# ConvFFN of a two-layer trunk: TensorE in source order, weight sums behind the previous pair, the first block's down products one pair later

## The chip, the cores and the metric

The kernel runs on one core of a Trainium2 chip. The metric is the device time of one execution in microseconds (us). A core has engines that each work through their own queue of instructions in order: TensorE (PE, with its weight loads as PEld), VectorE (DVE), ScalarE (ACT), GpSimd (POOL) and SyncE (SP). They meet at semaphores. PSUM, into which TensorE writes, has eight banks here, each a tile of 128 x 512 float32.

## The reference

The input is x of shape (1, 512, 1024), in float32. Two layers follow each other. Each is a token mixer and a feed-forward network (FFN); the change touches the FFN, which both layers have.

```python
for i in range(DEPTH):                       # DEPTH = 2
    h = rmsnorm(x, norm_mix_g[i])
    x = x + (gla_mixer(h, ...) if i % 2 == 0 else short_conv_mixer(h, ...))
    h = rmsnorm(x, norm_ffn_g[i])
    x = x + conv_ffn(h, ffn_w_up[i], ffn_conv_w[i], ffn_w_down[i])
return rmsnorm(x, final_norm_g)

def conv_ffn(h, w_up, conv_w, w_down):       # w_up 1024 x 5632, w_down 2816 x 1024
    up = causal_dwconv(h @ w_up, conv_w)     # three taps over the positions
    a, u = up[..., :D_FF], up[..., D_FF:]
    return (jax.nn.silu(a) * u) @ w_down
```

## The kernel before

**Tiling.** Channels lie on the 128 partitions and the 512 positions in the free dimension. The hidden layer of the FFN has 22 tiles j of 128 channels, each with a part a (`i = 0`) and a part u (`i = 1`). A product of float32 matrices is made of three matmuls on split operands: the high part (`h`) times the high part, high times low (`l`) and low times high. So each product of 128 x 128 weights comes as three matmuls.

**Weights.** Each weight tile is loaded raw by SP (L124, tile `wr`, a ring of 6 buffers), then split into `wh` and `wl` (mostly rings of 4). `halve` (L129) makes `wh` by a cast on ScalarE. It makes `wl` either by a subtraction on VectorE (L135) or, for units marked `added`, by a negated copy on ScalarE (L132) and an accumulating DMA that GpSimd issues (L133). `take` hands out one unit, and each call also starts the split of the unit three places further on. A raw buffer can be loaded again only when the split of what it held is done, and the loads wait in SP's queue in their order.

**Pairs.** Tiles j from 4 on are made in pairs of weight tiles (parts a and u of one j) by seven half-width products in place of eight. `seven_first` (step `s1`, 48 matmuls of 256 columns, PSUM tiles `updc` and `upab`) takes two units, `seven_last` (step `s2`, 36 matmuls) takes two more. The four units are sums and differences of the raw weights, made on VectorE in `forms`: `s` (L144) and L146 for the first unit, L150 and L151 for the later ones. In `seven_first` VectorE makes `e` (L671), the difference of two of the products. Behind `seven_last` VectorE and ScalarE make the two up tiles, the norm's factor (L696), the convolution (`conv3`, L365 to L367), the gate (L701, L702) and the split result `g<j>`.

**Plain tiles.** Tiles 0 to 3 are plain products of 24 matmuls of 512 columns (`up` both parts, `ua` part a, `ub` part u). Part u of tile 3 (`ub 3`) comes in the middle of pair 6.

**Down products.** The 22 tiles are cut into four blocks (0 to 5, 6 to 10, 11 to 15, 16 to 21). A step `dn b m` multiplies block b's tiles `g` by the weights of output tile m (18 matmuls of 512 columns for six tiles, 15 for five) and adds the result to `x[m]` (L715). The eight steps of a block are put between the pairs of the block behind it, by `ff_steps`. `dn 0 0` is called the first down group below. It is the first user of `g3`, the gate of tile 3.

**What sets the order.** The source says in which order the work is written down. Within that, the framework's scheduler decides each engine's order by its own idea of when operands are ready, so an instruction that stands later in the source can come earlier in a queue. `tc.issue_after(ins)` puts the instructions of a block behind `ins` on its engine; `tc.manual_schedule(engines=...)` keeps the source's order on the engines that it names.

The functions that the diff touches:

Of the kernel before, what the change touches and what calls it, by code (L numbers as in the profile page):

```python
# [18 lines left out]
KD = D // P  # L19
# [10 lines left out]
HALVED = 4  # L30
# [5 lines left out]
def trunk_kernel(ctx, tc, xT, w_qk, w_v, w_g, w_up_gate, b_gate, w_go, w_sc, w_so, w_up, w_dn,  # L36
                 smalls, ff_cw, out):
    nc = tc.nc
    V, S, G, PE = nc.vector, nc.scalar, nc.gpsimd, nc.tensor
# [9 lines left out]
    def ps(name):  # L49
        return psp.tile([P, T], F32, tag="ps", name=name)  # L50

    def wk(name, shape=(P, T), dt=F32, bufs=2, tag=None, pool=work):
        return pool.tile(list(shape), dt, tag=tag or name, name=name, bufs=bufs)
# [5 lines left out]
    def bt(tag, name, shape=(P, T), dt=F32):  # L59
        return big.tile(list(shape), dt, tag=tag, name=name)  # L60
# [20 lines left out]
    class Weights:  # L81
# [3 lines left out]
        def __init__(self):  # L85
            self.units, self.srcs, self.need, self.last = [], [], [], []
            self.raw, self.split, self.hold = {}, {}, {}
            self.paired, self.added = set(), set()

            self.anchors = ()  # L90
            self.nl = self.ns = self.ng = 0

        def add(self, src, added=False):
# [43 lines left out]
        def forms(self, n, q, h, l):  # L137


            ra, rb = self.raw[n], self.raw[n + 1]  # L140
            lo, hi = slice(0, T), slice(T, 2 * T)
            if q == 0:
                s3 = bt(f"b13{'hl'[n % 4 // 2]}", f"s{n}")
                V.tensor_add(s3, ra[:, lo], rb[:, lo])  # L144
                self.halve(h[:, lo], l[:, lo], s3)
                V.tensor_add(rb[:, lo], rb[:, lo], rb[:, hi])  # L146
                self.halve(h[:, hi], l[:, hi], rb[:, lo])
            elif q == 1:
                self.halve(h, l, ra)
                V.tensor_add(ra[:, lo], ra[:, lo], rb[:, lo])  # L150
                V.tensor_add(ra[:, hi], ra[:, hi], ra[:, lo])  # L151
            elif q == 2:
                self.halve(h, l, rb[:, hi])
            else:
                self.halve(h, l, ra)
# [38 lines left out]
        def take(self):  # L194

            for _ in range(2):
                if self.nl < len(self.srcs) and (self.nl < 6 or self.last[self.nl - 6] < self.ns):
                    self.load()
                    if self.nl not in self.paired:
                        break  # L200
            self.part()
            self.ng += 1
            return self.split.pop(self.ng - 1)

    W = Weights()
# [7 lines left out]
    def ff_steps():  # L213
        steps = [("up", 0), ("up", 1), ("ua", 2), ("s1", 4), ("ub", 2), ("s2", 4), ("s1", 5), ("ua", 3), ("s2", 5)]

        middle = [("ub", 3)]
        for b in range(1, len(BLOCKS)):
            j0, j1 = BLOCKS[b]
            dn = [("dn", b - 1, m) for m in range(KD)]
            for j in range(j0, j1):  # L220
                steps += [("s1", j), middle.pop() if j == j0 else dn.pop(0), ("s2", j)]
                if j1 - j < len(dn) or j == j0 and b > 1:
                    steps.append(dn.pop(0))
            middle = dn
        return steps + middle + [("dn", len(BLOCKS) - 1, m) for m in range(KD)]
# [15 lines left out]
    for i in range(KD):  # L241
        c, u, b = (w_sc[3 * i + n] for n in range(3))
# [76 lines left out]
    def split_to(src, name, tag, added=False):  # L319
        h = bt(f"{tag}h", f"{name}h", (P, T), F32R)  # L320
        l = bt(f"{tag}l", f"{name}l", (P, T), F32R)
        W.halve(h, l, src, added)
        return h, l
# [4 lines left out]
    def norm_parts(k, gi):  # L328
        h = bt(f"x{k}h", f"xh{k}", (P, T), F32R)
        l = bt(f"x{k}l", f"xl{k}", (P, T), F32R)  # L330
        a = S.activation(h, x[k], AF.Copy, scale=col(gi, k))
        v = V.scalar_tensor_tensor(l, x[k], col(gi, k), h.bitcast(F32), op0=ALU.mult, op1=ALU.subtract)
        xparts[k] = (h, l)
        return a.ins, v.ins
# [10 lines left out]
    def sum_parts(sq):  # L345
        h = wk("sh", dt=F32R, tag="sq")
        l = wk("sl", dt=F32R, tag="sq")
        S.copy(h, sq)
        V.tensor_sub(l, sq, h.bitcast(F32))
        return h, l  # L350

    def inv_rms_rows(parts, cnt):

        o = ps("sums")
        for i, a in enumerate(parts):
            PE.matmul(o, lhsT=onesr, rhs=a, start=i == 0, stop=i == 1)
        r = wk("r", bufs=2)
        S.activation(r, o, AF.Sqrt, bias=epst, scale=1.0 / cnt)  # L358
        V.reciprocal(r, r)  # L359
        return r  # L360
# [14 lines left out]
    for i, t in enumerate(als):  # L375
        b = slice(4 * i, 4 * i + 4)
# [4 lines left out]
    for k in range(1, KD):  # L381
        last = norm_parts(k, 0)
# [12 lines left out]
    sums = sum_parts(acc[0])  # L395
    q_ps.append(group("q2", xparts))
    W.part()
    r = inv_rms_rows(sums, D)
# [89 lines left out]
    kdt, st, sm = [None] * NH, [None] * NH, [None] * NH  # L488
# [157 lines left out]
    def product(out, ws, xs, first):  # L646
        for k in range(4):
            c = slice(k * P, (k + 1) * P)
            wh, wl = ws[0][:, c], ws[1][:, c]
            for i, (a, b) in enumerate(((wh, xs[k][0]), (wh, xs[k][1]), (wl, xs[k][0]))):  # L650
                PE.matmul(out, lhsT=a, rhs=b, start=first and k == 0 and i == 0, stop=k == 3 and i == 2,  # L651
                          skip_group_check=not first)


    lo, hi = slice(0, T // 2), slice(T // 2, T)

    def halves(w):
        return [(w[0][:, c:c + T], w[1][:, c:c + T]) for c in range(0, w[0].shape[1], T)]

    def cut(ks, c):  # L660
        return [tuple(p[:, c] for p in xparts[k]) for k in ks]

    def seven_first():

        dc, ab = ps("updc"), ps("upab")
        w1, w2 = halves(take())
        product(dc[:, lo], w1, tf[2], True)
        product(dc[:, hi], w2, tf[0], False)
        e = wk("e7", (P, HT), bufs=1)
        S.copy(e, dc[:, hi])  # L670
        V.tensor_sub(e, dc[:, lo], e)  # L671
        w1, w2 = halves(take())
        product(ab[:, lo], w1, cut(range(4), lo), True)
        product(ab[:, hi], w2, cut(range(4, 8), lo), False)
        u = wk("u", bufs=3)
        S.copy(u[:, lo], ab[:, hi])
        V.tensor_add(u[:, lo], u[:, lo], ab[:, lo])
        return dc, ab, e, u
# [11 lines left out]
        return u, u1  # L690

    def ffn_blocks(l, gnext):
        gp, cs, r = {}, {}, None

        def conv(j, i, u, src):
            V.tensor_mul(u, src, r)  # L696
            cs[j, i] = conv3(u, ffcw[:, l, i * NFF + j, :], f"c{i}", j == 0)

        def gate(j):
            a, u = cs.pop((j, 0)), cs.pop((j, 1))  # L700
            S.activation(a, a, AF.Silu)  # L701
            V.tensor_mul(u, u, a)  # L702
            gp[j] = split_to(u, f"g{j}", f"b{j % 11}", j not in SOON)

        for st in ff_steps():
            if st[0] == "dn":
                _, b, m = st
                last = b == len(BLOCKS) - 1
                if gnext is None and last and m == HALVED:
                    break  # L710
                part = group(f"dn{m}", [gp[j] for j in range(*BLOCKS[b])])
                if last and gnext is not None:
                    settle(m, part, gnext, False)
                else:
                    V.tensor_add(x[m], x[m], part)  # L715
                    if last:
                        norm_squares(m)
                continue
            step, j = st
            if step == "s1":  # L720
                begun = seven_first()
            elif step == "s2":
                for i, u in enumerate(seven_last(*begun)):
                    conv(j, i, u, u)
                gate(j)
            else:
                tiles = {"up": (0, 1), "ua": (0,), "ub": (1,)}[step]
                ups = {}
                for i in tiles:
                    ups[i] = group(f"up{i}", xparts)  # L730
                    if j == 0 and i == 0:
                        sums = sum_parts(acc[0])
                if j == 0:
                    r = inv_rms_rows(sums, D)
                for i in tiles:
                    conv(j, i, wk("u", bufs=3), ups[i])
                if 1 in tiles:
                    gate(j)
        return [gp[j] for j in range(*BLOCKS[-1])]

    ffn_blocks(0, 2)


    yparts = []
    for i in range(KD):
        if i in SC_SEVEN:
            begun = seven_first()
# [4 lines left out]
        else:  # L752
            cp = group("scc", xparts)
            if i == 0:
                sums = sum_parts(acc[0])
            up = group("scu", xparts)
            if i == 0:
                r = inv_rms_rows(sums, D)
# [11 lines left out]


    gp = ffn_blocks(1, None)

    wlast = {m: take() for m in range(HALVED, KD)}
# [69 lines left out]
    rb = last_rows(rl)  # L844
# [64 lines left out]
```

## Time and profile before

| | |
|---|---|
| three runs | 1096.43, 1097.52 (median) and 1100.97 us |
| profiled execution | 1096.32 us, its span 1094.6 us (1.7 us lie around it) |
| TensorE | 1079.5 us busy, 99% of the span |
| weight loads (PEld) | 967.8 us, 88% |
| VectorE | 851.9 us, 78% |
| ScalarE | 684.2 us, 63% |
| GpSimd | 128.2 us, 12% |

A busy time is the union of an engine's instruction spans. Matmuls overlap their predecessors, so the spacing of their starts, not their own duration, tells how fast TensorE goes. An idle stretch is shown with what ended it.

### The profile page before, as it was taken

To read this page: it belongs to the slowest core of one execution; us is meant where nothing else is said; L and a number is where in the kernel's file an instruction comes from. 1 tells how busy PE (TensorE), PEld (TensorE's weight loads), DVE (VectorE), ACT (ScalarE), POOL (GpSimd) and SP (SyncE) were. 2 spreads that over 40 slices of the span, in tenths; PEclk is the share of its full clock that TensorE was granted. 3 is DMA by queue.
4 is the path that set the end of the run, shared out by engine and by line. 5 is a ranking of instruction groups with operands and counts; after the bars stand their busy time and mean duration, and the time that the engine had idled before them with its cause. 6 is when DMAs were issued, how large, how long until landed. Compare 5 with 4: busy or idle time off the path is not lost.

```text
span 1094.6 us, 16998 instructions
## 1 busy us (share of the span) xinstructions
PE 1079.5 (99%) x6502; PEld 967.8 (88%) x6502; DVE 851.9 (78%) x1339; ACT 684.2 (63%) x1062; POOL 128.2 (12%) x160
## 2 busy tenths in 40 slices
PE   9999999999999999999999999999999999999997
PEld 7888888889899999999878998888989999999987
DVE  8874675789778989999678675477977888989954
ACT  7565765867656656666695455486755656666664
POOL 1000001101110111101111001011101011111120
PEclk9999999999999999999999999999999999999998
DMA  8332124865474564655897459386647556566573
GB/s 288 110 95 78 58 78 113 195 162 138 122 177 131 146 169 123 168 150 140 185 220 193 107 150 248 99 186 154 167 122 169 142 136 157 136 155 173 131 149 97
DMA packets 55958, 161.92 MB, mean 148 GB/s; under 512 B 6146, under 2 KB 8962, under 8 KB 55876
## 3 DMA queue, kind: packets, MB, share of 16 engines
q1 hardware_dynamic: 35428, 107.34, 31.1%
q0 software_dynamic: 20448, 53.49, 26.6%
q8 instruction: 51, 0.84, 0.3%
q14 instruction: 31, 0.25, 0.1%
HBM read 105.23 MB, written 2.10 MB: 98 GB/s over the span
## 4 chain that ended last, share of the span: by engine, by line
PE 68%; issue 3%; DMA 2%; DVE 1%; POOL 0%; ACT 0%; DVEq 0%; POOLq 0%; SPq 0%; ACTq 0%
PE updc L651 20%; PE dn L307 17%; PE upab L651 15%; PE scb L307 4%; PE so L307 4%; PE up L307 3%; PE dnl L307 2%; PE scu L307 1%; PE scc L307 1%; DMA wl<-wr 1%; DMA wr<-in_w_up 0%; POOL wl L133 0%; DVE wl L135 0%; DVE c L366 0%; DVE u L696 0%
## 5 line engine op out<-in xcount | busy, mean ns | idle before, releaser
L130 ACT CAST wh<-wr 128x1024 fp32r<-128x1024 f32 (+4 forms) x302 | 259.2, 863 | 187.3 <-PE upab L651 76.7
L135 DVE TENSOR_TENSOR wl<-wr,wh 128x512 fp32r<-128x512 f32 (+2 forms) x200 | 193.5, 981 | 60.0 <-ACT wh L130 59.2
L133 POOL DMA_DIRECT2D wl<-wr x102 | 89.2, 875 | 648.6 <-ACT wl L132 358.4
L365 ACT ACTIVATE c<-u,ffcw 128x512 f32<-128x512 f32 x88 | 59.3, 717 | 55.3 <-DVE u L696 55.3
L651 PE MATMUL upab<-xh,wh 128*128 128x256 f32 x328 | 92.8, 283 | 0.0
L651 PE MATMUL upab<-xl,wh 128*128 128x256 f32 x328 | 92.8, 283 | 0.0
L651 PE MATMUL upab<-xh,wl 128*128 128x256 f32 x328 | 92.8, 283 | 0.0
L132 ACT ACTIVATE wl<-wh 128x1024 fp32r<-128x1024 f32 (+2 forms) x102 | 90.8, 890 | 1.3
L366 DVE SCALAR_TENSOR_TENSOR c<-u,ffcw,c 128x511 f32<-128x511 f32 x88 | 62.4, 748 | 2.8 <-ACT c L365 2.6
L651 PEld LDWEIGHTS upab<-xh,wh 128*128 128x128 f32 x328 | 63.0, 192 | 0.0
L651 PEld LDWEIGHTS upab<-xl,wh 128*128 128x128 f32 x328 | 63.0, 192 | 0.0
L651 PEld LDWEIGHTS upab<-xh,wl 128*128 128x128 f32 x328 | 63.0, 192 | 0.0
L367 DVE SCALAR_TENSOR_TENSOR c<-u,ffcw,c 128x510 f32<-128x510 f32 x88 | 62.2, 746 | 0.0
L307 PE MATMUL up<-xh,wh 128*128 128x512 f32 x128 | 49.9, 390 | 0.0
L307 PE MATMUL up<-xl,wh 128*128 128x512 f32 x128 | 49.9, 390 | 0.0
L307 PE MATMUL up<-xh,wl 128*128 128x512 f32 x128 | 49.8, 389 | 0.0
L651 PE MATMUL updc<-xh,wh 128*128 128x256 f32 x164 | 46.4, 283 | 0.0
L651 PE MATMUL updc<-xl,wh 128*128 128x256 f32 x164 | 46.4, 283 | 0.0
L651 PE MATMUL updc<-xh,wl 128*128 128x256 f32 x164 | 46.4, 283 | 0.0
L696 DVE TENSOR_TENSOR u<-u,r 128x512 f32<-128x512 f32 x72 | 46.2, 684 | 0.0
L144 DVE TENSOR_TENSOR s<-wr,wr 128x512 f32<-128x512 f32 x41 | 28.2, 689 | 22.0 <-DMA wr<-in_w_up 15.3
L359 DVE RECIPROCAL r<-r 128x512 f32<-128x512 f32 x8 | 26.8, 3353 | 20.7 <-ACT r L358 20.7
(708 smaller groups left out, 3463.7 us busy)
## 6 DMA issues: line engine op xcount, KB each, us to landing
wr<-in_w_up SPq DMA_DIRECT2D x88, 512.0 KB, 3.9
wl<-wr POOLq DMA_DIRECT2D x38, 512.0 KB, 5.6
wr<-in_w_dn SPq DMA_DIRECT2D x32, 384.0 KB, 3.4
wl<-wr POOLq DMA_DIRECT2D x32, 384.0 KB, 4.1
wr<-in_w_sc SPq DMA_DIRECT2D x24, 512.0 KB, 4.4
wr<-in_w_dn SPq DMA_DIRECT2D x32, 320.0 KB, 3.2
wl<-wr POOLq DMA_DIRECT2D x32, 320.0 KB, 4.4
wr<-in_w_v SPq DMA_DIRECT2D x8, 512.0 KB, 3.7
```

What stands on the lines that cost most here:

```text
L130: S.copy(hh, src)
L132: S.activation(ll, hh.bitcast(F32), AF.Copy, scale=-1.0)
L133: G.dma_start(ll, src, accum_op=ALU.add)
L135: V.tensor_sub(ll, src, hh.bitcast(F32))
L144: V.tensor_add(s3, ra[:, lo], rb[:, lo])
L307: PE.matmul(out, lhsT=a, rhs=b, start=first and i == 0, stop=last and i == 2)
L359: V.reciprocal(r, r)
L365: a = S.activation(c, u, AF.Copy, scale=cw[:, 2:3])
L366: V.scalar_tensor_tensor(c[:, 1:], u[:, :T - 1], cw[:, 1:2], c[:, 1:], op0=ALU.mult, op1=ALU.add)
L367: v = V.scalar_tensor_tensor(c[:, 2:], u[:, :T - 2], cw[:, 0:1], c[:, 2:], op0=ALU.mult, op1=ALU.add)
L651: PE.matmul(out, lhsT=a, rhs=b, start=first and k == 0 and i == 0, stop=k == 3 and i == 2, skip_group_check=not first)
L696: V.tensor_mul(u, src, r)
```

## The change

Three things change, in both FFNs. VectorE's first sums of a pair (`s` and the second sum) are put behind `e` of the pair whose `seven_first` was written last (`W.pace`); both are now written before the first casts. In the list of steps the first block's down products begin one pair later: the steps were `s1 6, ub 3, s2 6, dn 0 0, s1 7, dn 0 1, s2 7, dn 0 2, ...` and are `s1 6, ub 3, s2 6, s1 7, dn 0 0, s2 7, dn 0 1, s1 8, ...`; from pair 10 on the list is as before. And all steps of an FFN but the last block's down products are written under `manual_schedule` for TensorE.

```diff
             if q == 0:
                 s3 = bt(f"b13{'hl'[n % 4 // 2]}", f"s{n}")
-                V.tensor_add(s3, ra[:, lo], rb[:, lo])
+                with ExitStack() as behind:
+                    if self.pace is not None:
+                        behind.enter_context(tc.issue_after(self.pace))
+                    V.tensor_add(s3, ra[:, lo], rb[:, lo])
+                    V.tensor_add(rb[:, lo], rb[:, lo], rb[:, hi])
                 self.halve(h[:, lo], l[:, lo], s3)
-                V.tensor_add(rb[:, lo], rb[:, lo], rb[:, hi])
                 self.halve(h[:, hi], l[:, hi], rb[:, lo])
...
                 steps += [("s1", j), middle.pop() if j == j0 else dn.pop(0), ("s2", j)]
-                if j1 - j < len(dn) or j == j0 and b > 1:
+                if (j1 - j < len(dn) if j > j0 else b > 1):
                     steps.append(dn.pop(0))
...
         S.copy(e, dc[:, hi])
-        V.tensor_sub(e, dc[:, lo], e)
+        W.pace = V.tensor_sub(e, dc[:, lo], e).ins
...
+        steps = ff_steps()
+        with tc.manual_schedule(engines={mybir.EngineType.PE}):
+            for st in steps[:-KD]:
+                take_step(st)
+        for st in steps[-KD:] if gnext is not None else steps[-KD:HALVED - KD]:
+            take_step(st)
```

On TensorE, this is the queue of before at the first down group of the first FFN (`dn0`); `updc` belongs to `s1 7`:

```order
L307 MATMUL dn0_2609<-g2h_2167,wl52_2490 128x512
L651 MATMUL updc_2634<-t150h_1654,wh53_2532 128x256
L651 MATMUL updc_2634<-t150l_1655,wh53_2532 128x256
L651 MATMUL updc_2634<-t150h_1654,wl53_2533 128x256
L307 MATMUL dn0_2609<-g3h_2526,wh52_2489 128x512
L651 MATMUL updc_2634<-t151h_1706,wh53_2532 128x256
```

Here is the queue of the change at the same group; `upab` is the last product of `s1 7`:

```order
L657 MATMUL upab_2610<-xh7_1799,wl53_2541 128x256
L313 MATMUL dn0_2673<-g0h_1926,wh54_2558 128x512
L313 MATMUL dn0_2673<-g0l_1927,wh54_2558 128x512
...
L313 MATMUL dn0_2673<-g2h_2169,wl54_2559 128x512
L313 MATMUL dn0_2673<-g3h_2532,wh54_2558 128x512
L313 MATMUL dn0_2673<-g3l_2533,wh54_2558 128x512
```

The whole of `s1 7` (48 matmuls) moved ahead of the group, and the group is no longer mixed with it. Outside these two groups, one in each FFN, the products stand on TensorE in the order of the list, before and after; the two mixed groups at the end of each FFN stay as they are.

On VectorE, this is the queue of before between pair 6's `u` (L677) and the gate of tile 3 (L702). `s51` is the first sum of pair 8, and `u_2518` starts the convolution of `ub 3`:

```order
L677 TENSOR_TENSOR u_2483<-u_2483,upab_2423 128x256
L135 TENSOR_TENSOR wl53_2533<-s47_2534,wh53_2532 128x512
L702 TENSOR_TENSOR c1_2411<-c1_2411,c0_2406 128x512
L135 TENSOR_TENSOR wl53_2533<-wr48_2351,wh53_2532 128x512
L144 TENSOR_TENSOR s51_2729<-wr51_2553,wr52_2555 128x512
L696 TENSOR_TENSOR u_2518<-up1_2486,r_1907 128x512
L135 TENSOR_TENSOR wl54_2558<-wr47_2349,wh54_2557 128x1024
L366 SCALAR_TENSOR_TENSOR c1_2520<-u_2518,ffcw_137,c1_2520 128x511
L150 TENSOR_TENSOR wr47_2349<-wr47_2349,wr48_2351 128x512
L367 SCALAR_TENSOR_TENSOR c1_2520<-u_2518,ffcw_137,c1_2520 128x510
L151 TENSOR_TENSOR wr47_2349<-wr47_2349 128x512
L702 TENSOR_TENSOR c1_2520<-c1_2520,c0_2345 128x512
```

This is the same stretch of the change; `s46` is the first sum of pair 7, whose raw tiles now come one place earlier in SP's queue, ahead of `dn 0 0`'s:

```order
L683 TENSOR_TENSOR u_2485<-u_2485,upab_2425 128x256
L149 TENSOR_TENSOR s46_2493<-wr46_2310,wr47_2312 128x512
L709 TENSOR_TENSOR c1_2413<-c1_2413,c0_2408 128x512
L150 TENSOR_TENSOR wr47_2312<-wr47_2312 128x512
L137 TENSOR_TENSOR wl52_2492<-s46_2493,wh52_2491 128x512
L137 TENSOR_TENSOR wl53_2541<-wr46_2310,wh53_2540 128x1024
L137 TENSOR_TENSOR wl52_2492<-wr47_2312,wh52_2491 128x512
L703 TENSOR_TENSOR u_2524<-up1_2488,r_1909 128x512
L155 TENSOR_TENSOR wr46_2310<-wr46_2310,wr47_2312 128x512
L156 TENSOR_TENSOR wr46_2310<-wr46_2310 128x512
L372 SCALAR_TENSOR_TENSOR c1_2526<-u_2524,ffcw_137,c1_2526 128x511
...
L709 TENSOR_TENSOR c1_2526<-c1_2526,c0_2349 128x512
```

The sum that stands ahead of tile 3's convolution is that of pair 7 now, and pair 8's sum stands behind `e` of pair 7.

On ScalarE, the casts of a pair's first units moved too. This is the queue of before ahead of the unit `wh105`, `wl105`, the weights of `dn 1 7`, behind pair 14's silu (L701):

```order
L130 CAST wh103_4161<-s79_4163 128x512
L670 COPY e7_4124<-updc_4094 128x256
L130 CAST wh103_4161<-wr80_3996 128x512
L365 ACTIVATE c1_4083<-u_4072,ffcw_137 128x512
L365 ACTIVATE c0_4078<-u_3990,ffcw_137 128x512
L130 CAST wh104_4190<-wr79_3994 128x1024
L676 COPY u_4155<-upab_4095 128x256
L701 ACTIVATE c0_4078<-c0_4078 128x512
L130 CAST wh105_4208<-wr81_4023 128x640
L130 CAST g14h_4089<-c1_4083 128x512
L132 ACTIVATE g14l_4090<-g14h_4089 128x512
L132 ACTIVATE wl105_4209<-wh105_4208 128x640
```

And this is the same stretch of the change:

```order
L676 COPY e7_4126<-updc_4096 128x256
L371 ACTIVATE c1_4085<-u_4074,ffcw_137 128x512
L371 ACTIVATE c0_4080<-u_3992,ffcw_137 128x512
L682 COPY u_4157<-upab_4097 128x256
L708 ACTIVATE c0_4080<-c0_4080 128x512
L132 CAST wh103_4163<-s79_4165 128x512
L132 CAST wh104_4192<-wr79_3996 128x1024
L132 CAST g14h_4091<-c1_4085 128x512
L132 CAST wh103_4163<-wr80_3998 128x512
L134 ACTIVATE g14l_4092<-g14h_4091 128x512
L132 CAST wh105_4210<-wr81_4025 128x640
L134 ACTIVATE wl105_4211<-wh105_4210 128x640
```

Three casts of pair 15's first two units went from ahead of the silu to behind it, ahead of `wl105`.

## Rows read from the trace of the kernel before

**Rows 1.** The page, busy time, share of the span and instructions of each engine.
```profile
PE 1079.5 (99%) x6502; PEld 967.8 (88%) x6502; DVE 851.9 (78%) x1339; ACT 684.2 (63%) x1062; POOL 128.2 (12%) x160
```

**Rows 2.** What TensorE waited for: us in total, times, longest.
```profile
PE dn L307 <- ACT g3h L130: 5.1, 2, 2.7
```

**Rows 3.** TensorE in order of time, first FFN: start, us, instruction, [idle before <-releaser].
```profile
284.92 0.40 PE L307 MATMUL dn<-g0h,wh 128*128 128x512 f32 x1
...
290.21 0.70 PE L307 MATMUL dn<-g3h,wh 128*128 128x512 f32 x1 [2.71 <-ACT g3h L130]
...
299.33 0.40 PE L307 MATMUL dn<-g0h,wh 128*128 128x512 f32 x1
```

**Rows 4.** The same view, starts of the third and the fourth down group.
```profile
307.75 0.40 PE L307 MATMUL dn<-g0h,wh 128*128 128x512 f32 x1
...
317.61 0.40 PE L307 MATMUL dn<-g0h,wh 128*128 128x512 f32 x1
```

**Rows 5.** The same view, first down group of the second FFN and the next group.
```profile
806.80 0.40 PE L307 MATMUL dn<-g0h,wh 128*128 128x512 f32 x1
...
811.78 0.50 PE L307 MATMUL dn<-g3h,wh 128*128 128x512 f32 x1 [2.40 <-ACT g3h L130]
...
821.10 0.40 PE L307 MATMUL dn<-g0h,wh 128*128 128x512 f32 x1
```

**Rows 6.** Stretches: length, busy time of each engine, granted clock (PEclk), DMA share, GB/s.
```profile
287.30:290.20 2.90, 0.20 (x2) 0.00 (x0) 2.90 (x7) 1.59 (x3) 0.86 (x1) 1.00 0.08 16
290.20:293.90 3.70, 3.69 (x12) 3.17 (x13) 3.70 (x7) 1.34 (x2) 0.00 (x0) 0.54 0.95 208
...
811.80:816.00 4.20, 4.20 (x13) 3.30 (x14) 4.20 (x8) 1.34 (x2) 0.00 (x0) 0.59 0.92 195
```

**Rows 7.** VectorE in order of time at the first down group of both FFNs.
```profile
277.49 0.42 DVE L677 TENSOR_TENSOR u<-u,upab 128x256 f32<-128x256 f32 x1
...
283.95 0.69 DVE L144 TENSOR_TENSOR s<-wr,wr 128x512 f32<-128x512 f32 x1 [4.24 <-issue]
284.56 0.68 DVE L696 TENSOR_TENSOR u<-up,r 128x512 f32<-128x512 f32 x1
285.16 1.22 DVE L135 TENSOR_TENSOR wl<-wr,wh 128x1024 fp32r<-128x1024 f32 x1
...
805.52 0.69 DVE L144 TENSOR_TENSOR s<-wr,wr 128x512 f32<-128x512 f32 x1 [3.93 <-DMA wr<-in_w_up]
```

**Rows 8.** ScalarE in order of time, the cast of tile 3's gate.
```profile
289.54 0.62 ACT L130 CAST g3h<-c 128x512 fp32r<-128x512 f32 x1 [1.27 <-DVE c L702]
```

**Rows 9.** The page's DMA issues: count, KB each, median us from issue to landing.
```profile
wr<-in_w_up SPq DMA_DIRECT2D x88, 512.0 KB, 3.9
...
wl<-wr POOLq DMA_DIRECT2D x32, 384.0 KB, 4.1
```

**Rows 10.** A stretch as in rows 6; it holds a pair and a plain tile.
```profile
254.00:270.00 16.00, 16.00 (x115) 15.04 (x114) 15.61 (x26) 11.69 (x18) 2.60 (x3) 1.00 0.71 183
```

**Rows 11.** Order of time at `dn 1 7`, first FFN: ScalarE, GpSimd, TensorE.
```profile
431.29 0.64 ACT L701 ACTIVATE c<-c 128x512 f32<-128x512 f32 x1 [0.70 <-DVE c L367]
...
434.41 0.72 ACT L132 ACTIVATE wl<-wh 128x640 fp32r<-128x640 f32 x1
...
437.51 1.06 ACT L130 CAST wh<-wr 128x1024 fp32r<-128x1024 f32 x1
...
435.50 1.11 POOL L133 DMA_DIRECT2D wl<-wr  x1
...
443.16 0.39 PE L307 MATMUL dn<-g6h,wl 128*128 128x512 f32 x1
```

**Rows 12.** Accumulating DMAs of low weights in 425 to 444 us, issue to landing.
```profile
DMA to landing us min/median/max: 4.4/5.0/5.7
```

**Rows 13.** As rows 11, second FFN's `dn 1 7`: GpSimd, TensorE.
```profile
957.58 0.87 POOL L133 DMA_DIRECT2D wl<-wr  x1
...
964.93 0.39 PE L307 MATMUL dn<-g6h,wl 128*128 128x512 f32 x1
```

More of the change, by code (lines that the diff above doesn't have):

```diff
@@ L90, in __init__ @@
             self.anchors = ()
+            self.pace = None
             self.nl = self.ns = self.ng = 0
@@ L692, in ffn_blocks @@
     def ffn_blocks(l, gnext):
-        gp, cs, r = {}, {}, None
+        gp, cs = {}, {}
+        r = sums = begun = None
         def conv(j, i, u, src):
@@ L703, in gate, with take_step @@
             gp[j] = split_to(u, f"g{j}", f"b{j % 11}", j not in SOON)
-        for st in ff_steps():
+        def take_step(st):
+            nonlocal r, sums, begun
             if st[0] == "dn":
@@ L708, in ffn_blocks @@
                 last = b == len(BLOCKS) - 1
-                if gnext is None and last and m == HALVED:
-                    break
                 part = group(f"dn{m}", [gp[j] for j in range(*BLOCKS[b])])
@@ L717, in ffn_blocks @@
                         norm_squares(m)
-                continue
+                return
             step, j = st
```

## The prediction

> **What bounds the kernel now.** I began with the page. TensorE is busy for 1079.5 of 1094.6 us [rows 1], so the end is set by TensorE, and only what it waits for, or what slows it, can be won. The waits of TensorE come next. The list is short, and its first line holds nearly all of the waiting in the body of the program: a down product waits for the cast of `g3`, twice, 5.1 us in all [rows 2]. The timeline of TensorE shows where. In the first FFN the first down group begins at 284.92, reaches `g3` and stands still for 2.71 us until 290.21; the next group begins at 299.33 [rows 3]. So the group and `s1 7` take 14.41 us. The same products, a group of 18 matmuls and an `s1` of 48, take 9.86 us undisturbed, from the third group's start to the fourth's [rows 4]. The excess is 4.55 us, more than the idle time. In the second FFN the distance is 821.10 - 806.80 = 14.30 us with 2.40 us of idle time [rows 5], an excess of 4.44 us.
>
> The stretches say what the rest is. In the 2.90 us from 287.30 TensorE is busy for 0.20 us. [...] So 5.11 us are waiting and 8.99 - 5.11 = 3.88 us are slow running behind it. [...] By the waits alone the sum below would be 5.1 us, with the clock it is 9.0.
>
> Why is `g3` late? VectorE's timeline answers. Behind `u` of pair 6 and three short operations it stands for 4.24 us in front of a first sum of raw weights (L144), and the convolution of `ub 3` (L696) stands behind that sum. In the second FFN the same sum waits for 3.93 us, and there the view names the load of a raw tile as what ended it [rows 7]. By the order, this sum is pair 8's, two pairs ahead of its use. The cast of `g3` then ends at 289.54 + 0.62 = 290.16 [rows 8].
>
> **The change part by part.**
>
> *Sums behind the pair ahead.* Pair 8's sum moves behind `e` of pair 7, and with it goes its wait for the load. In its place pair 7's sums stand ahead of the convolution of `ub 3`. Their raw tiles stand one place or more earlier in SP's queue than before, where these sums did not hold up this stretch, and a load takes 3.9 us to land [rows 9]; I take no wait for them. If that cover is gone, a wait of up to the 4.24 us of before comes back, and the margin found below just takes it. From the end of L677 at 277.91, six operations come ahead of L696 now, five of 0.69 us and one of 1.22 us [rows 7]: 4.67 us, so L696 starts at about 282.6. From its start to the end of the cast of `g3` it took 290.16 - 284.56 = 5.6 us before [rows 7, 8]. The order has the same work there with a smaller subtraction, so 5.6 us is an upper value, and `g3` is ready by 288.2. On ScalarE a cast of 1.06 us [rows 11] stands ahead of it, whose buffer is free at the end of `s2 6`, at 284.92; that is done by 286.0 and costs nothing.
>
> *One pair later.* The first group now starts behind `s1 7`. By columns `s1` is 48 x 256 of the 21,504 columns that take 9.86 us, 5.6 us, and nine down matmuls take 2.1 us. TensorE asks for `g3` at 284.92 + 5.6 + 2.1 = 292.6 in place of 287.5. The margin is 292.6 - 288.2 = 4.4 us. Each part alone would do: in the old place `g3` would come at 290.16 - 4.24 = 285.9 for 287.5, and in the new place with the old order it would come at 290.2 for 292.6. So both waits go, with the slow running behind them: 4.55 + 4.44 = 8.99 us. What the group needs besides is its low weights. Their buffer is free when `ub 3` ends, 36 matmuls (4.2 us) ahead of 284.92. A cast and a copy of about 0.9 us each (0.72 for 640 columns [rows 11], scaled to 768), an issue of about 1 and 4.1 us to land [rows 9] give 280.7 + 6.9 = 287.6, for 290.5. The later groups have the spacing that they had.
>
> *TensorE in source order.* Apart from the two first groups, its queue is the same. The order of products is not new, so I take 0. The price if the cover goes: in source order the rest of `s1 7` can't fill a wait at `g3`. Before, three matmuls of it stood ahead of the wait, 0.4 us for each FFN.
>
> *What moves on ScalarE.* Three casts of the next pair's first units now stand behind the silu and ahead of the low weights of a down group. This is so where that group follows an `s2` and an `s1` with no group between them: `dn 1 7` and `dn 2 5`, four places in the two FFNs. The casts take 0.62, 0.62 (the size of the cast of [rows 8]) and 1.06 us [rows 11], 2.3 us together. From the silu at 431.29 to the copy at 434.41 ScalarE had gaps that take up part of it, so the low weights come 0 to 2.3 us later. Their DMA was issued at 435.50, lands 4.4 to 5.7 us later [rows 12] and is used at 443.16 [rows 11]: a margin of 2.0 to 3.3 us. In the second FFN it is 964.93 - 957.58 less the same landing, 1.65 to 2.95 us [rows 13]. The cost is 0 to 0.65 us a place, 0 to 2.6 us in all. I take 0, since the median landing leaves at least 2.3 us everywhere, and keep 2.6 for the range.
>
> *Sum.* 1096.3 - 9.0 = 1087.3 us against the profiled execution. The median of the three runs lies 1.2 us above that execution, which would give 1088.5. I put 1088.0. Alone this case reaches from 1085.5 (another microsecond of small waits goes too) to 1090.
>
> **The rivals.** What a measurement of this kernel can tell from no change is about 0.5%, 5.5 us; faster then means below some 1092.
>
> Given back in part by late low weights: the four places above, and others where margins of 2 to 3 us shrink, wait for about 0.5 to 1 us each. For it speaks the order on ScalarE, against it the landing times. With 2 to 4 us lost, the time is 1090 to 1092.5.
>
> VectorE becomes the bound. In the stretch with a pair and a plain tile it is busy for 15.61 of 16.00 us [rows 10], and the change lets two halves of pairs follow each other there with no down group between. [...] Against it: the 4.24 us of standing still are gone from the same stretch, and that is more than was added. If it holds, each FFN keeps a wait of 1 to 3 us: about 1092.
>
> The change doesn't do what it says: `g3` was late for another reason too, and TensorE stands in the new place as long. For it speaks nothing that I found; 1096.
>
> Slower: low weights so late that the waits at the four places reach 2.4 us, the shorter of the two waits after which the clock fell. Each then costs about 4.5 us as the two waits of before did [rows 3 to 6], 18 us, and the time is 1105. It decides once the casts delay the DMA by 1.65 + 2.4 = 4.05 us or more; the three casts have 2.3 us.
>
> **How the numbers follow.** Both waits go: 0.62. Given back in part: 0.20, two thirds of it below 1092. VectorE the bound: 0.10, a third of it below 1092. No effect: 0.05. Slower: 0.03. That gives 0.62 + 0.13 + 0.03 = 0.78 for faster, 0.07 + 0.07 + 0.05 = 0.19 for the same and 0.03 for slower. The range from 1085 to 1093.5 holds the first case, the second, and more than half of the third, nearly 9 in 10.
>
> **What would show it.** In the changed trace no down product waits for the cast of `g3`. The first group of each FFN runs its 18 matmuls without a gap and at the full clock, and the stretch behind it is granted 1.00. VectorE's idle time in front of L149, the line of the first sum now, is small. The low weights of `dn 1 7` and `dn 2 5` land ahead of their first use. I am wrong if TensorE's waits name a low weight's DMA or `e` more than once or twice, if the granted clock falls at a new place, or if the first sum still waits for a load with `ub 3` behind it.

## The result, and the profile of the changed kernel

The changed kernel takes 1086.82 us (median of four runs, 1086.68 to 1086.95), the kernel before 1097.30 us (four runs, 1096.43 to 1100.97). The ratio is 0.9898, with a 95% interval from 0.9876 to 0.9921. The forecast was 1088.0 with a range from 1085 to 1093.5. The profiled execution took 1086.93 us with a span of 1085.2 us, 9.4 us less than that of before.

The page's busy times of the changed kernel:

```profile
PE 1075.6 (99%) x6502; PEld 965.2 (89%) x6502; DVE 855.7 (79%) x1339; ACT 684.3 (63%) x1062; POOL 127.8 (12%) x160
```

TensorE does the same 6502 matmuls in 3.9 us less busy time than in [rows 1]: from 290.6 to 299.0 us and from 807.0 to 815.6 us, at the first down groups, the granted clock is 1.00, where [rows 6] has 0.54 and 0.59. Its list of waits in full:

```profile
PE warm L76 <- DVE warm L64: 1.5, 1, 1.5
PE sums L808 <- DVE sq L799: 0.6, 1, 0.6
PE rb L821 <- DVE rl L815: 0.6, 1, 0.6
PE q L313 <- DVE xl L338: 0.2, 1, 0.2
PE q L313 <- ACT xh L337: 0.2, 1, 0.2
```

The line of [rows 2] is gone. What is left stands in the first 8.3 us and the last 9.5 us of the span. TensorE in order of time at the first down group of both FFNs, and at the groups behind:

```profile
290.60 0.40 PE L313 MATMUL dn<-g0h,wh 128*128 128x512 f32 x1
...
292.67 0.39 PE L313 MATMUL dn<-g3h,wh 128*128 128x512 f32 x1
...
299.02 0.40 PE L313 MATMUL dn<-g0h,wh 128*128 128x512 f32 x1
...
308.88 0.40 PE L313 MATMUL dn<-g0h,wh 128*128 128x512 f32 x1
...
807.13 0.40 PE L313 MATMUL dn<-g0h,wh 128*128 128x512 f32 x1
...
815.55 0.40 PE L313 MATMUL dn<-g0h,wh 128*128 128x512 f32 x1
```

`g3` is asked for at 292.67 and nothing stands in brackets. From the first group to the second it takes 8.42 us in both FFNs: 18 matmuls of 512 columns at 0.227 us and an `s2` of 36 at 0.120 us are 8.41. From the second group to the third, with an `s1`, it takes the 9.86 us of [rows 4]. The two excesses of 4.55 and 4.44 us are nil.

The stretches that answer to [rows 6] (length, busy times, granted clock, DMA share, GB/s):

```profile
287.30:290.20 2.90, 2.90 (x26) 2.90 (x26) 2.87 (x7) 2.37 (x4) 0.33 (x1) 1.00 0.81 250
290.20:293.90 3.70, 3.70 (x20) 3.13 (x19) 3.70 (x7) 1.71 (x4) 0.53 (x1) 1.00 0.84 220
```

The 3.70 us that held 12 matmuls at a granted 0.54 hold 20 at 1.00 (some of half width in both). VectorE, to be read against [rows 7], and ScalarE's cast, against [rows 8]:

```profile
276.91 0.42 DVE L683 TENSOR_TENSOR u<-u,upab 128x256 f32<-128x256 f32 x1
277.24 0.69 DVE L149 TENSOR_TENSOR s<-wr,wr 128x512 f32<-128x512 f32 x1
...
281.38 0.69 DVE L703 TENSOR_TENSOR u<-up,r 128x512 f32<-128x512 f32 x1
...
290.08 0.42 DVE L677 TENSOR_TENSOR e<-updc,e 128x256 f32<-128x256 f32 x1
```

```profile
286.14 0.63 ACT L132 CAST g3h<-c 128x512 fp32r<-128x512 f32 x1
```

The first sum follows without idle time, tile 3's convolution starts at 281.38 (before: 284.56), and the cast of `g3` ends at 286.77, 5.9 us ahead of its use.

Last, the low weights of `dn 1 7`, GpSimd's issue and TensorE's first use, in both FFNs:

```profile
432.56 0.86 POOL L135 DMA_DIRECT2D wl<-wr  x1 [0.53 <-DVE wr L155]
...
948.88 0.87 POOL L135 DMA_DIRECT2D wl<-wr  x1 [0.50 <-DVE wr L155]
```

```profile
438.53 0.39 PE L313 MATMUL dn<-g6h,wl 128*128 128x512 f32 x1
...
955.06 0.39 PE L313 MATMUL dn<-g6h,wl 128*128 128x512 f32 x1
```

From issue to use there are 5.97 and 6.18 us now, against 7.66 [rows 11] and 7.35 [rows 13]. The weights come 1.7 and 1.2 us later in relation to their use, and still in time.

### The profile page after: what moved, and what is told of

Its sections match the earlier page's. It is cut to its first block, busy times and chain, and to the rows that moved or that the text cites. A ratio compares the mean times of both kernels' runs of the same rounds, so it can differ in the third digit from the quotient of the medians.

```text
span 1085.2 us, 17009 instructions
## 1 busy us (share of the span) xinstructions
PE 1075.6 (99%) x6502; PEld 965.2 (89%) x6502; DVE 855.7 (79%) x1339; ACT 684.3 (63%) x1062; POOL 127.8 (12%) x160
## 4 chain that ended last, share of the span: by engine, by line
PE 98%; DMA 0%; DVE 0%; ACT 0%; SPq 0%; DVEq 0%; issue 0%
PE updc L657 22%; PE dn L313 21%; PE upab L657 16%; PE up L313 8%; PE g L313 4%; PE scb L313 4%; PE v L313 4%; PE so L313 4%; PE go L313 4%; PE k L313 2%; PE q L313 2%; PE dnl L313 2%; PE scc L313 2%; PE scu L313 2%; PE o L536 1%; PE o L538 0%
## 5 line engine op out<-in xcount | busy, mean ns | idle before, releaser
L137 DVE TENSOR_TENSOR wl<-wr,wh 128x1024 fp32r<-128x1024 f32 (+2 forms) x200 | 193.1, 982 | 60.5 <-ACT wh L132 60.2
L708 ACT ACTIVATE c<-c 128x512 f32<-128x512 f32 x44 | 27.8, 632 | 31.4 <-DVE c L373 31.4
L721 DVE TENSOR_TENSOR x<-x,dn 128x512 f32<-128x512 f32 x52 | 35.7, 686 | 14.4 <-PE dn L313 13.4
```

Source lines behind the costliest of these rows:

```text
L137: V.tensor_sub(ll, src, hh.bitcast(F32))
```

## The experiments

### Each part alone

Four kernels leave parts of the change out. "Pace" is the placing of the sums behind `e`. With the later start and the pace but no manual schedule, the queues of TensorE, VectorE and ScalarE are those of the change word for word, so that kernel was not run.

The pace alone (against the change):

```diff
-                if (j1 - j < len(dn) if j > j0 else b > 1):
+                if j1 - j < len(dn) or j == j0 and b > 1:
...
-        with tc.manual_schedule(engines={mybir.EngineType.PE}):
-            for st in steps[:-KD]:
-                take_step(st)
+        for st in steps[:-KD]:
+            take_step(st)
```

> The sums behind `e` alone; the list of steps and the scheduler's order of TensorE stay as before. Theory (VectorE's standing at pair 8's sum made `g3` late): without it `g3` is ready near 285.9 us and is asked for at 287.5, so no wait at `dn 0 0`, clock 1.00 behind it, time 1086.5 to 1088. Rival (the group has to move, since VectorE has too much to do there anyway): `dn 0 0` still waits 1 to 2.5 us for `g3` in each FFN, time 1090 to 1096.

The later start alone (against the kernel before):

```diff
-                if j1 - j < len(dn) or j == j0 and b > 1:
+                if (j1 - j < len(dn) if j > j0 else b > 1):
```

> The first block's down products one pair later alone; sums as before, TensorE under the scheduler (its order comes out word for word as in the change). Theory: VectorE still stands some 4 us at pair 8's sum or another, `g3` still comes near 290, but is asked for near 292.6, so no wait: 1086.5 to 1088. Rival (VectorE's standing is handed on to `e` of pair 7, which the low half of `s2 7` needs near 294.7; in the changed kernel it ends at 290.5, and 4 us later that is just the time it is asked for): a wait of 0.5 to 1.5 us in each FFN, with little or no fall of the clock, 1088 to 1090.

TensorE's source order alone (against the kernel before):

```diff
+        with tc.manual_schedule(engines={mybir.EngineType.PE}):
+            for st in steps[:-KD]:
+                take_step(st)
```

> TensorE in source order alone; sums and list of steps as before. Theory: both waits for `g3` stay, each 0.4 us longer, because no matmuls of `s1 7` stand ahead of them: 2.7 to 3.1 us of idle time each and the clock falls again behind them; 1096.5 to 1098. Rival (the source order takes part in the gain): below 1093.

The pace and the source order, without the later start (against the change):

```diff
-                if (j1 - j < len(dn) if j > j0 else b > 1):
+                if j1 - j < len(dn) or j == j0 and b > 1:
```

> The sums behind `e` and TensorE in source order; the first block's down products stay where they were. Theory: `g3` ready near 286 us for 287.5, no wait, 1086.5 to 1087.5, the same as the sums alone, and the low weights of `dn 1 7` and `dn 2 6` have the margins of the change, since these places are not touched by the later start. Rival (the later start is needed for the last microsecond): 1088 or more, with a short wait at `g3`.

Measured beside 17 runs of the kernel before (median 1097.14, 1093.57 to 1099.60):

| kernel | median us | ratio, 95% interval | wait at `dn 0 0`, first FFN |
|---|---|---|---|
| pace alone | 1086.91 | 0.9909 [0.9893, 0.9925] | none |
| later start alone | 1086.88 | 0.9909 [0.9893, 0.9925] | none |
| source order alone | 1100.91 | 1.0033 [1.0021, 1.0046] | 5.19 for `g3h`, 0.42 for `g3l` |
| pace and source order | 1087.81 | 0.9915 [0.9900, 0.9931] | 0.24 for `g3l` |

Each of the two parts brings all of the gain, as the prediction had it. The source order brings none and, without the later start, costs. Beside the pace it costs 0.9 us: the second half `g3l` is asked for 0.24 us too soon in both FFNs, where the scheduler would have put three matmuls of `s1 7`, and the distance from the first group to the second is 10.39 and 10.40 us, for 10.03 in both FFNs with the pace alone, which makes 0.7 of the 0.9. By itself it costs 3.8 us, far above the 0.8 expected. TensorE in order of time, source order alone:

```profile
292.02 0.80 PE L310 MATMUL dn<-g3h,wh 128*128 128x512 f32 x1 [5.19 <-ACT g3h L132]
293.24 0.79 PE L310 MATMUL dn<-g3l,wh 128*128 128x512 f32 x1 [0.42 <-DVE g3l L137]
```

And the later start alone did not do it in the expected way. VectorE with that part alone:

```profile
280.48 0.68 DVE L146 TENSOR_TENSOR s<-wr,wr 128x512 f32<-128x512 f32 x1
```

The sum ahead of tile 3's convolution (here too pair 8's) waits for nothing, the convolution starts behind it at 281.08, and the cast of `g3` ends at 286.98, not near 290. The rival fell with it: `e` of pair 7 is not late either.

### What held the load

So the question became why a raw tile was late at all. Three views of the kernel before: GpSimd's accumulating DMA of `dn 0 0`'s low weights, SP's load of pair 8's second raw tile, and the page of the stretch from 274 to 281 us with the time from issue to landing of each.

```profile
274.55 0.86 POOL L133 DMA_DIRECT2D wl<-wr  x1 [6.13 <-DVE e L671]
```

```profile
280.21 0.33 SPq L124 DMA_DIRECT2D wr<-in_w_up  x1
```

```profile
wr<-in_w_up SPq DMA_DIRECT2D x1, 512.0 KB, 3.7
wl<-wr POOLq DMA_DIRECT2D x1, 384.0 KB, 5.6
```

274.55 + 5.6 = 280.15, and the load is issued at 280.21; 280.21 + 3.7 = 283.9, and the sum starts at 283.95 [rows 7]. The accumulating DMA reads the raw tile itself. The ring has six buffers, and the loads stand in the order `dn 0 0`, pair 7 (two), `dn 0 1`, `dn 0 2`, pair 8 (two): the seventh, pair 8's second, goes into the buffer of the first. With the later start the order is `ub 3`, pair 7 (two), `dn 0 0`, `dn 0 1`, pair 8 (two): pair 8's second tile follows into the buffer of `ub 3`, which is free sooner, and its load is issued at 273.05. The next kernel changes this order alone, in the kernel before, so that `dn 0 2`'s tile, wanted much later, goes into the buffer of `dn 0 0`:

```diff
+        def add_pair_ahead(self, a, b):
+            n = len(self.srcs) - 1
+            self.srcs[n:n] = [a, b]
+            self.last[n:n] = [None, None]
+            self.need[-1] = n + 2
...
-                pair = W.add_pair(w_up[l, 2 * st[1]], w_up[l, 2 * st[1] + 1])
+                ahead = W.add_pair_ahead if st[1] == BLOCKS[1][0] + 2 else W.add_pair
+                pair = ahead(w_up[l, 2 * st[1]], w_up[l, 2 * st[1] + 1])
```

> The kernel before with one change: the raw tiles of pair 8 are loaded ahead of the raw tile of `dn 0 2`; steps, sums and the scheduler's freedom on TensorE stay. In the kernel before, the load of pair 8's second raw tile goes into the buffer that `dn 0 0`'s raw tile held, and that one is free only when the accumulating DMA of `dn 0 0`'s low weights is issued, near 280.2 us; so the load lands near 283.9 and VectorE stands at pair 8's sum until then. Theory (that ring is the cause): with the pair one buffer further ahead it lands before 279, VectorE does not stand, `g3` is ready near 286 for 287.5: 1086.5 to 1088, as the changed kernel, with neither of its parts. Rival (the load is late for another reason, the DMA queue or its own 4 to 5 us of transfer): the wait at the sum and at `g3` stays, 1094 to 1099.

It takes 1086.81 us (ratio 0.9908 [0.9892, 0.9924]), with no wait in either FFN. SP's load of pair 8's second tile, its load of `dn 0 2`'s tile, and VectorE in this kernel:

```profile
272.90 1.25 SPq L135 DMA_DIRECT2D wr<-in_w_up  x1
```

```profile
281.04 0.33 SPq L135 DMA_DIRECT2D wr<-in_w_dn  x1
```

```profile
279.57 0.69 DVE L155 TENSOR_TENSOR s<-wr,wr 128x512 f32<-128x512 f32 x1
```

The ring is the cause. The sum waits for nothing, and tile 3's convolution starts at 280.90. Pair 8's load is issued 7.3 us sooner than before, and the tile that now follows into `dn 0 0`'s buffer waits in its stead: the accumulating DMA, issued at 274.49, lands after 6.5 us, at 280.99, and `dn 0 2`'s load follows at 281.04. The buffer comes free at that landing; the expectation calls the same time the issue. The rival, a load that is late by its own transfer, is out: here it took 6.2 us to land, longer than the 3.7 before, and VectorE's sum did not wait for it. The wait came once in each FFN, and a buffer that was not free stood behind it. The cure was the order of the six; a seventh was not tried.

### Whether the transfers set the size of the wait

The kernel before and the source order alone were profiled once more, unchanged.

> The kernel before, unchanged, profiled again. In its first profile the accumulating DMA of `dn 0 0`'s low weights landed 5.6 us after its issue and the load behind it 3.7 us after its own. Theory (the wait at `g3`, and with it the time of a run, follows the landing of these two transfers): if they land sooner or later by some amount, the wait at `g3` moves by the same amount, and the span by a little more where the clock falls. Rival (the waits are the same in all runs and the spread of 1093.6 to 1099.8 us has another cause): the wait is again 2.7 and 2.4 us whatever the time.

> The kernel with the source order alone, profiled again; it waited 5.2 and 4.0 us for `g3`, where 3.1 at most were expected. Up to the cast of `g3` the queues of all engines but TensorE are those of the kernel before, word for word. Theory (0.4 us a wait is the lost cover, the rest is the scatter of two transfers, which landed 1.8 us later): the two transfers land at other times than in its first profile, and the wait follows them. Rival (the source order makes these transfers slow in some systematic way): the load lands again near 285.7 us and the waits are again 5.2 and 4.0 us.

One time each: 1093.82 and 1100.54 us. The sums on VectorE, from the kernel before again, the source order again, and its first profile:

```profile
283.36 0.69 DVE L144 TENSOR_TENSOR s<-wr,wr 128x512 f32<-128x512 f32 x1 [3.74 <-issue]
```

```profile
285.15 0.69 DVE L146 TENSOR_TENSOR s<-wr,wr 128x512 f32<-128x512 f32 x1 [5.44 <-issue]
```

```profile
285.76 0.69 DVE L146 TENSOR_TENSOR s<-wr,wr 128x512 f32<-128x512 f32 x1 [6.37 <-DMA wr<-in_w_up]
```

The first `g3` product started at 289.62, 291.41 and 292.02, and at 290.21 in [rows 3]: 6.26 us behind the sum in all four, and in the second FFNs too. So the wait is the sum's start plus 6.26 less the time at which TensorE asks, and it follows the two transfers one for one. They differ between runs (5.6 + 3.7 us before, 6.7 us for the first alone in the source order's first profile, and the load issued at 280.97). Why they landed 1.2 to 2.4 us later in the first FFN of both profiles of the source order stays open; the queues of the other engines are the same up to there, and from 274 to 278 us the DMA moved 219 and 223 GB/s, for 299 in both profiles of before. So the rival that the source order itself slows them is not out.

But later transfers are not all that the source order costs. In the second FFN of its repeat they were not late:

```profile
809.34 0.40 PE L310 MATMUL dn<-g0h,wh 128*128 128x512 f32 x1
...
813.86 0.80 PE L310 MATMUL dn<-g3h,wh 128*128 128x512 f32 x1 [2.29 <-ACT g3h L132]
...
825.16 0.40 PE L310 MATMUL dn<-g0h,wh 128*128 128x512 f32 x1
```

```profile
817.90:821.90 4.00, 4.00 (x24) 3.81 (x23) 3.64 (x5) 1.04 (x1) 0.00 (x0) 0.69 0.22 84
```

```profile
815.80:819.80 4.00, 4.00 (x33) 3.92 (x32) 2.88 (x5) 2.55 (x4) 0.00 (x0) 0.98 0.23 85
```

`g3` comes 4.52 us behind the group's start, sooner than the 4.98 us of [rows 5], yet the way to the next group takes 15.82 us for 14.30. TensorE waits 2.72 us in place of 2.40 (0.43 of it for `g3l`) and loses 3.24 us besides in place of 2.04: the granted clock is still 0.69 in the second 4 us, where the first profile of before has 0.98 (last line, from that profile). So the source order costs 1.5 us here. 0.3 us of it is idle time (0.8 for the lost cover, half of it at `g3h` and half at `g3l`, less the 0.46 by which `g3` comes sooner), and the rest is slower running. Why the clock stays low for longer was not tested.

The repeat of the kernel before shows how much one wait can differ in price. In its first FFN:

```profile
284.83 0.40 PE L307 MATMUL dn<-g0h,wh 128*128 128x512 f32 x1
...
289.62 0.50 PE L307 MATMUL dn<-g3h,wh 128*128 128x512 f32 x1 [2.20 <-ACT g3h L130]
...
297.58 0.40 PE L307 MATMUL dn<-g0h,wh 128*128 128x512 f32 x1
```

```profile
289.60:293.60 4.00, 3.86 (x21) 3.27 (x22) 4.00 (x8) 1.85 (x3) 0.00 (x0) 1.00 0.89 200
```

The wait is 0.51 us shorter than in [rows 3], but the excess is 2.89 us in place of 4.55: the granted clock stayed at 1.00. In the second FFN the wait is 2.35 us and the excess 4.60.

### What a wait costs

The next two kernels put a wait back into `dn 0 0` of the changed kernel, made by GpSimd (17 clears in the first FFN and 32 in the second; the other kernel has 24 and 50):

```diff
+    zero = const.tile([P, P], F32R, name="zero")
...
+                    PE.matmul(part, lhsT=zero[:, 0:P], rhs=gs[0][0], start=True, stop=False)
+                    for _ in range((17, 32)[l]):
+                        G.memset(zero.bitcast(F32), 0.0)
+                    for k, wt in enumerate(take()):
+                        if k == 3:
+                            PE.matmul(part, lhsT=zero[:, 0:P], rhs=gs[0][0], start=False, stop=False)
+                        mm3(part, wt, gs[k], False, k == len(gs) - 1)
```

> The changed kernel, with a wait put back at the old place in `dn 0 0`, ahead of `g3`, that has nothing to do with `g3`: GpSimd clears a tile of zeros again and again behind the group's first matmul, and a matmul with that tile (it adds zero) stands ahead of `g3`. 17 clears in the first FFN, an estimate of 0.9 us of idle time, and 32 in the second, 3.0 us. All other operands are ready by then. The four extra matmuls cost 0.9 us. Theory (3.9 of the 9.0 us were the lower clock behind the waits): the stretch behind the long wait is granted 0.5 to 0.6 and costs 1.9 us more than the wait; for the short one either 0 or up to 1.9. Time 1086.8 + 0.9 + 3.9 + 1.9 = 1093.5, up to 1095.4. Rival (the slow running before came from late operands, `g3l` and the gates behind it): only the waits are paid, 1091.6, and the clock stays at 1.00.

> The same with 24 clears in the first FFN, an estimate of 1.9 us of idle time, and 50 in the second, 5.5 us. Theory: the lower clock costs about 1.9 us behind each wait, the same behind the longer one as behind the shorter: 1086.8 + 0.9 + 7.4 + 3.8 = 1098.9. If the loss grows with the wait, as 3.88 lost for 5.11 waited would have it in proportion, 5.6 lost: 1100.7. Rival (only the waits): 1095.1.

They took 1102.40 and 1109.67 us. The estimates of the waits were low: 17 clears of the same tile took 4.41 us, 0.26 each. TensorE in the first of them:

```profile
290.81 0.40 PE L722 MATMUL dn<-g0h,zero 128*128 128x512 f32 x1
...
296.16 0.50 PE L727 MATMUL dn<-g0h,zero 128*128 128x512 f32 x1 [2.90 <-POOL zero L724]
...
304.44 0.40 PE L315 MATMUL dn<-g0h,wh 128*128 128x512 f32 x1
...
812.42 0.40 PE L722 MATMUL dn<-g0h,zero 128*128 128x512 f32 x1
...
822.50 0.80 PE L727 MATMUL dn<-g0h,zero 128*128 128x512 f32 x1 [7.65 <-POOL zero L724]
...
831.04 0.40 PE L315 MATMUL dn<-g0h,wh 128*128 128x512 f32 x1
```

Undisturbed, this distance is 8.42 + 0.45 for the two added matmuls, 8.87 us. 304.44 - 290.81 - 8.87 = 4.76 us lost for 2.90 us of idle time, and 831.04 - 812.42 - 8.87 = 9.75 for 7.65. The stretches behind the waits, in the first kernel and in the second:

```profile
296.20:300.20 4.00, 4.00 (x13) 3.27 (x14) 1.05 (x2) 1.30 (x2) 0.86 (x1) 0.65 0.75 193
822.50:826.50 4.00, 4.00 (x10) 3.14 (x10) 0.00 (x0) 0.00 (x0) 0.00 (x0) 0.50 0.24 45
```

```profile
829.80:833.80 4.00, 4.00 (x9) 3.14 (x10) 0.00 (x0) 0.00 (x0) 0.00 (x0) 0.50 0.01 4
```

No operand but the zeros was waited for, and the granted clock fell as in [rows 6], here to 0.65, 0.50 and 0.50. So the slow running is the clock's, and the rival of late operands is out. Worked out in the same way, the waits of 4.73 and 12.36 us in the second kernel lost 7.53 and 15.36 us. With the waits for `g3` of the kernel before (two profiles) and of the source order alone (two profiles, the waits for `g3h` and `g3l` together), and with the granted clock of the 4 us behind each:

| kernel | wait, us | lost besides, us | granted clock |
|---|---|---|---|
| before | 2.20 | 0.69 | 1.00 |
| before | 2.35 | 2.25 | 0.70 |
| before | 2.40 | 2.04 | 0.60 |
| before | 2.71 | 1.84 | 0.57 |
| source order alone | 2.72 | 3.24 | 0.50 |
| clears | 2.90 | 1.86 | 0.65 |
| source order alone | 4.67 | 3.34 | 0.50 |
| source order alone | 4.70 | 3.33 | 0.57 |
| clears | 4.73 | 2.80 | 0.50 |
| source order alone | 5.61 | 2.75 | 0.50 |
| clears | 7.65 | 2.10 | 0.50 |
| clears | 12.36 | 3.00 | 0.50 |

The loss does not grow in proportion to the wait, and two waits of nearly the same length can differ in it by 1.6 us. 4.76 + 9.75 + 0.9 = 15.4 us accounts for the 15.6 us by which the first kernel is slower than the change.

### Where late low weights begin to cost

The changed kernel, with the negated copy of three low weights repeated:

```diff
-                S.activation(ll, hh.bitcast(F32), AF.Copy, scale=-1.0)
+                for _ in range(again):
+                    S.activation(ll, hh.bitcast(F32), AF.Copy, scale=-1.0)
...
+                if st[1:] in ((1, 7), (2, 5), (2, 6)):
+                    W.again[len(W.units)] = (2, 4)[l]
```

> The changed kernel with the negated copy of the low weights of `dn 1 7`, `dn 2 5` and `dn 2 6` made twice in the first FFN (0.7 us later) and four times in the second (2.2 us later). In the changed kernel these weights land 0.7 to 1.4 us ahead of their first use. Theory (late low weights are the next limit, and it begins where that margin ends): no wait in the first FFN; in the second three waits of about 1.2, 0.8 and 1.4 us, 3.4 us in all, with the lower clock behind them perhaps 2 to 4 more: 1090 to 1094. Rival (ScalarE's gaps and the later places in its queue take the delay up, or the copies delay other casts first): 1086.8 to 1088, or a wait at another place.

It takes 1091.46 us (ratio 0.9949 [0.9931, 0.9968]), 4.6 us more than the change. What TensorE waited for, and three of the four places in order of time:

```profile
PE dn L316 <- DMA wl<-wr: 3.5, 4, 1.3
```

```profile
499.98 0.49 PE L316 MATMUL dn<-g11h,wl 128*128 128x512 f32 x1 [0.30 <-DMA wl<-wr]
...
956.95 0.50 PE L316 MATMUL dn<-g6h,wl 128*128 128x512 f32 x1 [1.07 <-DMA wl<-wr]
...
1019.40 0.50 PE L316 MATMUL dn<-g11h,wl 128*128 128x512 f32 x1 [1.34 <-DMA wl<-wr]
```

In the second FFN the waits came at the three places: 1.07 us at `dn 1 7`, 1.34 at `dn 2 5` and the rest of the 3.5, nearly 0.8, at `dn 2 6`, 3.2 in all for the 3.4 expected. In the first FFN `dn 2 5` waited 0.30 us, where no wait was expected. Behind all four the clock stayed at a granted 1.00 over 4 us, here behind the longest of them:

```profile
1019.40:1023.40 4.00, 4.00 (x21) 3.43 (x22) 2.45 (x6) 3.80 (x6) 0.86 (x1) 1.00 0.59 147
```

Four waits of 3.5 us together cost 4.6 us by the medians and 4.2 by the spans (1089.4 for 1085.2), 0.2 to 0.3 us besides for each.

## Why the prediction was right, and where its reasons were not

**The waits and their price.** Right. 8.99 us were to go, and both excesses went to nil. That 3.88 of them were the clock rests on [rows 6], with 0.54 and 0.59 granted behind the two waits; the waits without `g3`, with 0.50 to 0.65 granted behind them, show it. The size holds for this profile of before and not for each run: the repeat lost 0.69 + 2.25 = 2.94 us in this way.

**The time.** 1087.3 was the sum against the profiled execution, which measured 1086.93. That they lie so near is in part luck. In the second layer's mixer a product waited for its low weights before, and waits no more:

```profile
562.20 0.50 PE L307 MATMUL scc<-xh,wl 128*128 128x512 f32 x1 [0.57 <-DMA wl<-wr]
```

From the third group of the first FFN to the first of the second there are 499.05 us in this profile (307.75 to 806.80) and 498.15 in the repeat of before (306.00 to 804.15), where the wait is missing too. So 0.9 us of the gain came with a wait that comes and goes without the change. Against it the end of the program, from the sums of the last norm on, took 8.9 us in place of 8.4.

The step up to 1088.0 was the wrong one: it carried the spread of the kernel before into the changed one. How the two profiles of before, 1096.32 and 1093.82 us, differ is shown: 1.5 us lie at the two waits for `g3` (excesses of 4.55 and 4.44 us for 2.89 and 4.60), most of it not idle time (5.11 us for 4.55) but clock (1.00 granted behind the repeat's first wait, for 0.57), and 0.9 us at the wait in the mixer. That the spread of the other runs, 1093.6 to 1099.8 us, has the same sources is argued. Without the waits four runs lie within 0.3 us.

**The cause of the late `g3`.** Half right. VectorE did stand at pair 8's sum with tile 3's convolution behind it. The prediction took the sum's place in VectorE's queue for the cause; behind it was the load's place in the ring of raw buffers, held by the accumulating DMA of `dn 0 0`. The step that failed is "in the new place with the old order it would come at 290.2 for 292.6": it came at 286.98, since moving the group also moves its raw tile, and pair 8's second tile then follows into another buffer. A step in the list is a place in three queues; the prediction followed TensorE's, and of SP's only the place of pair 7's tiles.

**When `g3` is ready.** 288.2 was forecast as an upper value for the change, 286.77 was measured. Tile 3's convolution started at 281.38 for 282.6: the six operations ahead of it took 4.05 us for 4.67, since those of 0.69 us start 0.60 apart, and `u` ended 0.6 us sooner than before.

**Each part alone would do.** Right, but with less to spare than forecast for the pace: the cast of `g3` ends there at 286.94 and is asked for at 287.25, where 285.9 for 287.5 was forecast. For the later start it came true by luck: the reason given failed, and the buffer did it.

**TensorE's source order.** 0 in the whole change was right. The price without cover, 0.4 us in each FFN, fits beside the pace (0.36 by the distances between groups). By itself the source order cost 1.9 us in each FFN by the medians. The lost cover, 0.4 us for `g3h` and 0.4 for `g3l`, is only a part of it; the profiles show besides slower running for longer behind the wait and, in three of four places, later transfers. What each is worth in the median run stays open.

**Low weights.** 0 to 2.3 us later was forecast, 1.7 and 1.2 were measured, at no cost. The rival "given back in part" did not come. The last experiment puts its edge less than 0.7 us further on, at `dn 2 5` first, one of the places named.

**VectorE as the bound.** Did not come. `e` of pair 7 ends at 290.50 and its successor on TensorE starts at 294.71, 4.2 us later. No run shows the waits of 1 to 3 us on which its 1092 stood; none came at this place.

## What to carry to other kernels

When an engine stands at a load, ask first which transfer still held the buffer that the load goes into: here one place in a ring of six was worth as much as either rewrite. An order of steps sets the order of products, of loads and of buffer releases at once, so follow all three. And a wait of TensorE can cost more than its idle time: here the waits from 2.35 us on cost 1.8 to 3.3 us besides, one of 2.20 us 0.7, and four of up to 1.34 us 0.2 to 0.3 each.

## What the runs showed of the hardware

Where the granted clock fell behind a wait, to 0.50 to 0.70 over the 4 us behind it, 1.8 to 3.3 us were lost besides, for waits from 2.35 to 12.36 us; behind one wait of 2.20 us it stayed at 1.00 and 0.7 us were lost. Behind the waits for clears of 4.73, 7.65 and 12.36 us the granted clock was 0.50 over 4 us. An accumulating DMA of 384 KB held the raw tile that it reads until it landed: it landed 5.6, 6.5 and 6.7 us behind its issue in the first profile of the kernel before, with the loads alone reordered and in the first profile of the source order alone, and in each the next load into that buffer was issued within 0.1 us of the landing. GpSimd's 17 clears of one 128 x 128 tile, one behind the other, took 4.41 us, 0.26 us each.
